# An RG-LRU and attention trunk: another order of the first loads, squares and adds, and the first block's convolution by halves

## The chip, the cores and the metric

The kernel runs on 1 core of a Trainium2 chip. The metric is the device time of one execution in microseconds (us); lower is better. The engines are TensorE (PE; weight loads are listed as PEld), VectorE (DVE), ScalarE (ACT), GpSimd (POOL) and SyncE (SP), whose queue issues nearly all DMAs.

## The reference

One sequence of 1024 positions, width 1024, float32, goes through two pre-norm residual layers. The change lies in the first, the RG-LRU layer, of width 1536 in 12 blocks of 128:

```python
def rms_norm(x, g):
    y = xf * lax.rsqrt(jnp.mean(xf * xf, axis=-1, keepdims=True) + EPS)
    return (y * g).astype(x.dtype)

def lru_mixer(h, w_in, conv_w, conv_b, wa, ba, wx, bx, a_param, w_out):
    u = h @ w_in
    xb, gate = u[..., :LRU_WIDTH], u[..., LRU_WIDTH:]
    xc = causal_depthwise_conv(xb, conv_w, conv_b)      # 4 taps
    r = jax.nn.sigmoid(block_diag_linear(xc, wa, ba))
    i = jax.nn.sigmoid(block_diag_linear(xc, wx, bx))
    log_a = -LRU_C * r * jax.nn.softplus(-a_param)
    a = jnp.exp(log_a)
    bterm = jnp.sqrt(-jnp.expm1(2.0 * log_a)) * (i * xc)
    _, hs = lax.associative_scan(combine, (a, bterm), axis=1)
    return (hs * jax.nn.silu(gate)) @ w_out
```

The second layer is forgetting attention with 16 heads of 64; the change does not touch its code.

## The kernel before, in words

Everything is held transposed: features on the 128 partitions, positions along a row. The 1024 positions are two halves of 512 (`halves`); x is 16 tiles `xs[h][k]` of 128x512, 256 KB each, h the half and k one of KT = 8 feature tiles. A printed name as x03 is half 0, k = 3. Precision is kept by splitting: each x tile, scaled by the norm's g (gnt), becomes hh (cast on ACT) and hl (the rest, on VectorE, L242); each weight tile of 128x512 (four k) becomes wh (cast on ACT, L88) and wl (the rest, L99, on VectorE or POOL). A product is three matmuls per k: hh with wh, hh with wl, hl with wh.

The norm's factor is applied after the products. `square_x` squares the x tiles on ACT (L252) and adds them up in m2 (`acc`, L254; the buffers of the squares are the later tiles th and ti); `first_row(h)` multiplies m2 by ones into row, takes the root on ACT (L261) and the reciprocal on VectorE (L262): rs. Then us = ups times rs (`conv`, L279), xc = four taps of us (one on ACT, L280, three on VectorE, L283), xch and xcl its split; `gates` multiplies those with the split gate weights wgh and wgl; `softplus` is a chain of operations on 128x12 values on VectorE that ends with c2 and nc2, which `recur` reads on ACT (L329, L330); `silu` scales gps by rs, takes tanh and writes sg; `recur` scans; `outputs` splits the result into yh and yl, and `project_out` multiplies them with the output weights (ops) and adds into x.

The loop runs over the 12 blocks. Block 0 makes its u product (ups) and its gate product (gps) while x is still arriving; block 1 makes ups for both halves with the row of the second half between; later blocks use two-bank PSUM tiles (tag S, two of them), so the third block's ups (ups_549 before) takes the place that block 0's ups or gps held. Loads come in the order of the string in the loop over steps (n gnt, u and g half a weight column of 256 KB each, x one x tile, p the small parameters pct); all go through SP's queue in order.

The order on each engine is not the order of the code: a tile scheduler interleaves the instructions by its own costs and due times, and each engine then works through its queue in order. `issue_after` holds instructions back until a named one is issued.

Of the kernel before, what the change touches and what calls it, by code (L numbers as in the profile page):

```python
# [11 lines left out]
F32 = mybir.dt.float32  # L12
F32R = mybir.dt.float32r
BF16 = mybir.dt.bfloat16
AF = mybir.ActivationFunctionType
ALU = mybir.AluOpType

P = 128
SEQ = 1024
HALF = 512  # L20
KT = 8
NB = 12
# [16 lines left out]
def trunk(ctx: ExitStack, tc: tile.TileContext, xt, w0, wg, wo0, pc, gn, gf, w1, wv, wf, bf, wo1, out):  # L39
    nc = tc.nc  # L40

    def pool(name, bufs, **kw):
        return tc.tile_pool(name=name, bufs=bufs, **kw)
# [2 lines left out]
    const.tile([P, 32], F32, name="pad0")  # L46
    ctx.enter_context(pool("edge", 1, side="right")).tile([P, 56], F32, name="pad1")
    dram = ctx.enter_context(pool("dram", 1, space=DRAM))
    ctx.enter_context(pool("gap", 1)).tile([P, 24], F32, name="pad2")
    hpool = ctx.enter_context(pool("hT", 16))  # L50
    wpool = ctx.enter_context(pool("w", 4))
    ps = ctx.enter_context(pool("ps", 2, space=PSUM))
# [45 lines left out]
    def to_lo(lo, src, hi, eng):  # L98
        return eng.tensor_tensor(lo, src, f32(hi), ALU.subtract)  # L99
# [14 lines left out]
    def weights(src, parts=wpool, lo_eng=nc.gpsimd):  # L114

        for k in range(0, src.shape[1], 4):
            n = min(4, src.shape[1] - k)
            yield from split_weights([(src[:, k : k + n], slice(0, P))], (n, P), nc.scalar, lo_eng, parts)
# [13 lines left out]
    def drain(gen):  # L132
        for _ in gen:
            pass
# [45 lines left out]
    with ExitStack() as l0:  # L180
# [8 lines left out]
        def long(tag, dtype=F32, bufs=1):  # L189
            return tmp.tile([P, SEQ], dtype, tag=tag, name=tag, bufs=bufs)  # L190
# [28 lines left out]

        xs = [[xpool.tile([P, HALF], F32, name=f"x{h}{k}") for k in range(KT)] for h in range(2)]  # L220
        first = ([], [])
        early = [weights(w0[0], lo_eng=nc.vector), weights(w0[NB], lo_eng=nc.gpsimd)]
        k = 0
        for step in "nuxxgxuxgxxpxxxxxxxxxx":
            if step == "n":
                nc.sync.dma_start(gnt, gn)
            elif step == "p":
                nc.sync.dma_start(pct, pc)
            elif step in "ug":
                first["ug".index(step)].extend(itertools.islice(early["ug".index(step)], 4))  # L230
            else:
                nc.sync.dma_start(xs[k // KT][k % KT], xt[k // KT, :, k % KT])
                k += 1
# [3 lines left out]
        def split_x(h, layer=0):  # L237
            for k, (hi, lo) in enumerate((raw, hT)[layer][h]):
                g_ = gnt[:, layer, k : k + 1]
                x = xs[h][k]  # L240
                to_hi(hi, x, nc.scalar, scale=g_)
                nc.vector.scalar_tensor_tensor(lo, x, g_, f32(hi), ALU.mult, ALU.subtract)  # L242
                yield
# [4 lines left out]
        def square_x(h):  # L248
            to = acc[:, halves[h]]
            for k in range(KT):  # L250
                z = sq[k % 4] if k else to
                nc.scalar.activation(z, xs[h][k], AF.Square)  # L252
                if k:
                    nc.vector.tensor_tensor(to, to, z, ALU.add)  # L254
                yield

        def first_row(h):
# [6 lines left out]
        def rms_row(parts, rs, *rms):  # L264
            return inv_rms(parts, ps.tile([P, HALF], F32, tag="O", name="sscol")[:, : HALF // P], rs, *rms)

        for _ in zip(split_x(0), square_x(0)):
            pass


# [2 lines left out]
        def product(pt, h, w):  # L273
            gemm(pt, zip(w, raw[h]))

        def conv(n, ups):
            us, xc = long("us"), long("xc", bufs=2)
            for pt, cs in zip(ups, halves if len(ups) == 2 else (slice(0, SEQ),)):
                nc.vector.tensor_tensor(us[:, cs], pt, rs[:, cs], ALU.mult)  # L279
            nc.scalar.activation(xc, us, AF.Identity, bias=cb[:, n : n + 1], scale=cw[3][:, n : n + 1])  # L280
            for d in range(1, 4):
                w_ = cw[3 - d][:, n : n + 1]
                tap = nc.vector.scalar_tensor_tensor(xc[:, d:], us[:, : SEQ - d], w_, xc[:, d:], ALU.mult, ALU.add)  # L283
            xh, xl = long("xch", F32R), long("xcl", F32R)
            to_hi(xh, xc, nc.scalar)
            to_lo(xl, xc, xh, nc.vector)
            wt = wpool.tile([P, 4, P], F32, tag="wf", name="wgf", bufs=3)[:, :2]
            nc.sync.dma_start(wt, wg[n])
            wgh = tmp.tile([P, 2, P], F32R, tag="wgh", name="wgh")
            wgl = tmp.tile([P, 2, P], F32R, tag="wgl", name="wgl")  # L290
            to_hi(wgh, wt, nc.vector)
            to_lo(wgl, wt, wgh, nc.vector)
            state[n] = dict(xc=xc, x=(xh, xl), w=(wgh, wgl), tap=tap)

        def gates(n):

# [81 lines left out]
        for n in range(NB):  # L378
# [14 lines left out]
            if n == 0:  # L393
                gps = held[0] = two_banks("gps")
                product(gps[:, 0], 0, first[1])
                first_row(0)
                for _ in zip(split_x(1), square_x(1)):
                    pass
            else:
                gates(n - 1)  # L400
                if n > 1:
                    with tc.issue_after(state[n - 1]["last"].ins):
                        outputs(n - 2)
            product(ups[1], 1, wu)
            if n == 0:
                row, rooted, done = first_row(1)
                product(gps[:, 1], 1, first[1])
                both = ups
            conv(n, both)
            if n == 0:  # L410
                with tc.issue_after(rooted.ins), tc.issue_after(done.ins):
                    softplus()
                drain(silu(state[0], held.pop(0)))
            if n % 2 and n > 1:
                fill = itertools.chain(fill, project_out((n - 3) // 2))
            take(fill, 4)
# [684 lines left out]
```

## Time and profile before

| what | value |
|---|---|
| median of three runs | 1130.3 us (1128.25 to 1131.4) |
| the profiled execution | 1132.74 us, its span 1130.9 us |
| TensorE busy | 1112.0 us, 98% of the span |
| VectorE, ACT, POOL busy | 67%, 52%, 15% |
| mean granted TensorE clock | 0.995 |
| read from HBM | 63.30 MB |

The profile is of one execution. Its rows give start, duration, engine, line, operation and tiles by the program's names; what stands in brackets is the idle time ahead of an instruction and what ended it. Overlapping matmuls are shown with their whole duration, so the spacing of their starts is the rate. A row that ends in x2 stands for two instructions that follow each other, with the time from the first's start to the last's end.

### The profile page before, as it was taken

Reading aid. Unit: us, or ns where it says so; the run is one execution under the profiler, and the core shown is the slowest. Engines: PE = TensorE matmul, PEld = TensorE weight load, DVE = VectorE, ACT = ScalarE, POOL = GpSimd, SP = SyncE. Lnnn points to the kernel's source line nnn. Section 1 sums busy time; section 2 is a strip of 40 time slices with the busy share of each in tenths; the row PEclk is TensorE's granted clock in tenths of the full one; section 3 lists DMA queues with packets and bytes.
Section 4 is the critical chain, followed back from the end, with each engine's and each line's share of the span. In section 5 each row is a group of like instructions: output and inputs, shape, how many; then the busy total and the mean of one; then the engine's idle time right before and its main releaser. Section 6 shows DMA issues by size and latency. Waiting matters only on the chain.

```text
span 1130.9 us, 15754 instructions
## 1 busy us (share of the span) xinstructions
PE 1112.0 (98%) x5681; PEld 937.3 (83%) x5681; DVE 762.2 (67%) x1271; ACT 589.6 (52%) x1077; POOL 165.6 (15%) x105
## 2 busy tenths in 40 slices
PE   9999999999999999999999999999999999999997
PEld 7786888888888887988888888888888888878886
DVE  7789756876568789666676466763666645676645
ACT  8387445354453666455555355553555534554435
POOL 1312112121121202330110100101001010010110
PEclk9999999999999999999999999999999999999999
DMA  6111121111211114443334124252142421665445
GB/s 216 52 42 52 43 61 38 52 52 42 61 37 52 56 57 144 124 123 103 99 89 119 52 84 109 75 123 62 58 120 85 110 81 52 182 180 157 151 149 186
DMA packets 63702, 105.43 MB, mean 93 GB/s; under 512 B 9508, under 2 KB 24484, under 8 KB 63624
## 3 DMA queue, kind: packets, MB, share of 16 engines
q1 hardware_dynamic: 63624, 104.42, 31.3%
q8 instruction: 45, 0.74, 0.3%
q14 instruction: 33, 0.27, 0.1%
HBM read 63.30 MB, written 15.93 MB: 70 GB/s over the span
## 4 chain that ended last, share of the span: by engine, by line
PE 87%; DVE 4%; ACT 2%; DMA 2%; issue 2%; POOL 1%; SPq 0%; POOLq 0%; ACTq 0%
PE gps L57 32%; PE ops L57 15%; PE ups L57 10%; PE vps L57 7%; PE S L57 6%; PE O L57 6%; PE pt L61 5%; PE turn L57 3%; PE gate L57 2%; POOL wl L99 1%; DMA wf<-in_w 1%; DVE sq L167 1%; ACT wh L88 1%; DVE x L470 0%; DMA x<-in_xt 0%
## 5 line engine op out<-in xcount | busy, mean ns | idle before, releaser
L57 PE MATMUL gps<-hh,wh 128*128 128x512 f32 x576 | 228.6, 397 | 1.0 <-DVE qkl L582 1.0
L57 PE MATMUL gps<-hl,wh 128*128 128x512 f32 x576 | 226.0, 392 | 0.0
L57 PE MATMUL gps<-hh,wl 128*128 128x512 f32 x576 | 226.0, 392 | 0.0
L88 ACT CAST wh<-wf 128x512 fp32r<-128x512 f32 (+2 forms) x156 | 94.6, 607 | 146.6 <-PE gps L57 49.2
L707 ACT ACTIVATE p<-S,m 128x128 f32<-128x128 f32 (+7 forms) x128 | 94.9, 741 | 135.2 <-DVE m L702 134.1
L99 POOL TENSOR_TENSOR wl<-wf,wh 128x512 fp32r<-128x512 f32 (+1 forms) x60 | 100.7, 1685 | 389.4 <-ACT wh L88 332.5
L99 DVE TENSOR_TENSOR pl<-pt,ph 128x512 fp32r<-128x512 f32 (+1 forms) x198 | 98.8, 540 | 81.7 <-ACT ph L88 81.3
L57 PEld LDWEIGHTS gps<-hl,wh 128*128 128x128 f32 x576 | 108.4, 188 | 23.8
L57 PEld LDWEIGHTS gps<-hh,wh 128*128 128x128 f32 x576 | 108.6, 189 | 20.2 <-DVE qkl L582 1.2
L57 PEld LDWEIGHTS gps<-hh,wl 128*128 128x128 f32 x576 | 108.9, 189 | 19.7 <-POOL wl L99 0.7
L702 DVE CUSTOM_DVE_ANT_0 S<-S,mask 128x128 f32<-128x128 f32 (+7 forms) x128 | 97.3, 761 | 30.2 <-PE S L57 25.8
L734 POOL TENSOR_TENSOR sg<-sg,recb 64x1024 f32<-64x1024 f32 (+1 forms) x17 | 38.8, 2282 | 460.8 <-DMA recb<-recd 400.8
L88 ACT CAST ph<-pt 128x512 fp32r<-128x512 f32 (+1 forms) x198 | 83.6, 473 | 30.6 <-PE pt L61 25.3
L57 PE MATMUL S<-T,U 96*128 96x512 f32 (+7 forms) x384 | 91.7, 348 | 2.4 <-ACT p L707 2.4
L99 DVE TENSOR_TENSOR wl<-wf,wh 128x512 fp32r<-128x512 f32 x96 | 70.0, 733 | 26.5 <-ACT wh L88 25.8
L369 DVE TENSOR_TENSOR x<-x,ops 128x512 f32<-128x512 f32 x80 | 54.1, 682 | 48.1 <-PE ops L57 48.1
L57 PEld LDWEIGHTS S<-T,U 128*128 128x128 f32 (+1 forms) x384 | 68.3, 189 | 15.6 <-ACT p L707 3.6
L61 PE MATMUL pt<-ident,p 128*128 128x128 f32 x576 | 79.4, 273 | 0.0
L57 PE MATMUL ups<-hh,wh 128*128 128x512 f32 x192 | 76.6, 400 | 1.7 <-ACT hh L90 1.0
L61 PEld LDWEIGHTS pt<-ident,p 128*128 128x128 f32 x576 | 67.4, 141 | 12.4 <-issue 2.2
L57 PE MATMUL vps<-wh,hh 128*128 128x256 f32 (+1 forms) x256 | 74.6, 292 | 3.0 <-DVE sg L673 2.1
L57 PE MATMUL ups<-hh,wl 128*128 128x512 f32 x192 | 76.0, 396 | 1.5 <-POOL wl L99 1.5
(176 smaller groups left out, 2260.0 us busy)
## 6 DMA issues: line engine op xcount, KB each, us to landing
wf<-in_w SPq DMA_DIRECT2D x100, 256.0 KB
wf<-in_wo SPq DMA_DIRECT2D x64, 128.0 KB
U<-qkh SPq DMA_DIRECT2D x64, 128.0 KB
T<-qkh SPq DMA_DIRECT2D x28, 256.0 KB
x<-in_xt SPq DMA_DIRECT2D x16, 256.0 KB
x1d<-x SPq DMA_DIRECT2D x16, 256.0 KB
wf<-in_wv SPq DMA_DIRECT2D x16, 256.0 KB
U<-qkl SPq DMA_DIRECT2D x32, 128.0 KB
```

The source lines that it names most:

```text
L57: pe[0] = nc.tensor.matmul(*args, **kw)
L61: pe[0] = nc.tensor.transpose(*args)
L88: nc.scalar.copy(hi, src)
L99: return eng.tensor_tensor(lo, src, f32(hi), ALU.subtract)
L167: eng.tensor_tensor(parts[0], parts[0], sq, ALU.add)
L369: nc.vector.tensor_tensor(x, x, pt, ALU.add)
L702: nc.vector.tensor_tensor_reduce(S[:, :n], S[:, :n], mask[:, SEQ - n :], -1.0, -NEG, ALU.add, ALU.min, accum_out=m)
L707: seen[0] = nc.scalar.activation(p, S[:, :n], AF.Exp, bias=m, scale=-1.0, accum_out=sums[:, i : i + 1])
L734: nc.gpsimd.tensor_tensor(sg, sg, recs[hd // 2][rows, cs], ALU.mult)
```

## The change

1. pad2 is 40 floats wide instead of 24, which moves the tiles placed behind it by 64 bytes in each partition.
2. The wl tiles of block 0's gate weights are made by VectorE instead of POOL.
3. The loads come in another order: g's first half ahead of x01, u's and g's second halves behind x03, pct last.
4. Splitting the first half's x is no longer interleaved with squaring it: the first half is split, then the second half is split with the first half squared, then the second half is squared, then the first half's row follows. The first half's adds are on POOL; the second's stay on VectorE.
5. Block 0's convolution and silu are done by halves: taps, xch and xcl 512 wide each; the silu is held back until the second root is issued. Taps are in a function of their own (`taps`), used by all blocks.

The instructions are as many as before but for the halves; on TensorE the same matmuls stand in another order in the first 900 or so.

```diff
--- before.py
+++ after.py
@@ -46,7 +46,7 @@
     const.tile([P, 32], F32, name="pad0")
     ctx.enter_context(pool("edge", 1, side="right")).tile([P, 56], F32, name="pad1")
     dram = ctx.enter_context(pool("dram", 1, space=DRAM))
-    ctx.enter_context(pool("gap", 1)).tile([P, 24], F32, name="pad2")
+    ctx.enter_context(pool("gap", 1)).tile([P, 40], F32, name="pad2")
     hpool = ctx.enter_context(pool("hT", 16))
     wpool = ctx.enter_context(pool("w", 4))
     ps = ctx.enter_context(pool("ps", 2, space=PSUM))
@@ -219,9 +219,9 @@
 
         xs = [[xpool.tile([P, HALF], F32, name=f"x{h}{k}") for k in range(KT)] for h in range(2)]
         first = ([], [])
-        early = [weights(w0[0], lo_eng=nc.vector), weights(w0[NB], lo_eng=nc.gpsimd)]
+        early = [weights(w0[0], lo_eng=nc.vector), weights(w0[NB], lo_eng=nc.vector)]
         k = 0
-        for step in "nuxxgxuxgxxpxxxxxxxxxx":
+        for step in "nuxgxxxugxxxxxxxxxxxxp":
             if step == "n":
                 nc.sync.dma_start(gnt, gn)
             elif step == "p":
@@ -251,7 +251,7 @@
                 z = sq[k % 4] if k else to
                 nc.scalar.activation(z, xs[h][k], AF.Square)
                 if k:
-                    nc.vector.tensor_tensor(to, to, z, ALU.add)
+                    (nc.vector if h else nc.gpsimd).tensor_tensor(to, to, z, ALU.add)
                 yield
 
         def first_row(h):
@@ -264,7 +264,7 @@
         def rms_row(parts, rs, *rms):
             return inv_rms(parts, ps.tile([P, HALF], F32, tag="O", name="sscol")[:, : HALF // P], rs, *rms)
 
-        for _ in zip(split_x(0), square_x(0)):
+        for _ in split_x(0):
             pass
 
 
@@ -273,24 +273,37 @@
         def product(pt, h, w):
             gemm(pt, zip(w, raw[h]))
 
-        def conv(n, ups):
+        def conv(n, ups, parts=(slice(0, SEQ),)):
             us, xc = long("us"), long("xc", bufs=2)
+            xh, xl = long("xch", F32R), long("xcl", F32R)
             for pt, cs in zip(ups, halves if len(ups) == 2 else (slice(0, SEQ),)):
                 nc.vector.tensor_tensor(us[:, cs], pt, rs[:, cs], ALU.mult)
-            nc.scalar.activation(xc, us, AF.Identity, bias=cb[:, n : n + 1], scale=cw[3][:, n : n + 1])
-            for d in range(1, 4):
-                w_ = cw[3 - d][:, n : n + 1]
-                tap = nc.vector.scalar_tensor_tensor(xc[:, d:], us[:, : SEQ - d], w_, xc[:, d:], ALU.mult, ALU.add)
-            xh, xl = long("xch", F32R), long("xcl", F32R)
-            to_hi(xh, xc, nc.scalar)
-            to_lo(xl, xc, xh, nc.vector)
+                if len(parts) < len(ups):
+                    continue
+                taps(n, us, xc, cs)
+            if len(parts) < len(ups):
+                taps(n, us, xc, parts[0])
+            for cs in parts:
+                to_hi(xh[:, cs], xc[:, cs], nc.scalar)
+                to_lo(xl[:, cs], xc[:, cs], xh[:, cs], nc.vector)
             wt = wpool.tile([P, 4, P], F32, tag="wf", name="wgf", bufs=3)[:, :2]
             nc.sync.dma_start(wt, wg[n])
             wgh = tmp.tile([P, 2, P], F32R, tag="wgh", name="wgh")
             wgl = tmp.tile([P, 2, P], F32R, tag="wgl", name="wgl")
             to_hi(wgh, wt, nc.vector)
             to_lo(wgl, wt, wgh, nc.vector)
-            state[n] = dict(xc=xc, x=(xh, xl), w=(wgh, wgl), tap=tap)
+            state[n] = dict(xc=xc, x=(xh, xl), w=(wgh, wgl), tap=last_tap[0])
+
+        last_tap = [None]
+
+        def taps(n, us, xc, cs):
+            nc.scalar.activation(xc[:, cs], us[:, cs], AF.Identity, bias=cb[:, n : n + 1], scale=cw[3][:, n : n + 1])
+            for d in range(1, 4):
+                w_ = cw[3 - d][:, n : n + 1]
+                to = slice(max(cs.start, d), cs.stop)
+                last_tap[0] = nc.vector.scalar_tensor_tensor(
+                    xc[:, to], us[:, to.start - d : to.stop - d], w_, xc[:, to], ALU.mult, ALU.add
+                )
 
         def gates(n):
 
@@ -393,9 +406,11 @@
             if n == 0:
                 gps = held[0] = two_banks("gps")
                 product(gps[:, 0], 0, first[1])
+                for _ in zip(split_x(1), square_x(0)):
+                    pass
+                for _ in square_x(1):
+                    pass
                 first_row(0)
-                for _ in zip(split_x(1), square_x(1)):
-                    pass
             else:
                 gates(n - 1)
                 if n > 1:
@@ -406,11 +421,12 @@
                 row, rooted, done = first_row(1)
                 product(gps[:, 1], 1, first[1])
                 both = ups
-            conv(n, both)
+            conv(n, both, halves if n == 0 else (slice(0, SEQ),))
             if n == 0:
                 with tc.issue_after(rooted.ins), tc.issue_after(done.ins):
                     softplus()
-                drain(silu(state[0], held.pop(0)))
+                with tc.issue_after(rooted.ins):
+                    drain(silu(state[0], held.pop(0), halves))
             if n % 2 and n > 1:
                 fill = itertools.chain(fill, project_out((n - 3) // 2))
             take(fill, 4)
```

How the change moves instructions. First the start: VectorE from its first wl on, before; hl is named with the x tile that it is made of, m2 is the sum of squares.

```order
L99 TENSOR_TENSOR wl_138<-wf_136,wh_137 128x512
L242 SCALAR_TENSOR_TENSOR hl_179<-x00_119,gnt_101,hh_178 128x512
L242 SCALAR_TENSOR_TENSOR hl_181<-x01_120,gnt_101,hh_180 128x512
L254 TENSOR_TENSOR m2_210<-m2_210,th_211 128x512
L242 SCALAR_TENSOR_TENSOR hl_183<-x02_121,gnt_101,hh_182 128x512
L254 TENSOR_TENSOR m2_210<-m2_210,ti_212 128x512
L99 TENSOR_TENSOR wl_153<-wf_151,wh_152 128x512
L242 SCALAR_TENSOR_TENSOR hl_185<-x03_122,gnt_101,hh_184 128x512
```

The same place in the changed program:

```order
L99 TENSOR_TENSOR wl_138<-wf_136,wh_137 128x512
L242 SCALAR_TENSOR_TENSOR hl_179<-x00_119,gnt_101,hh_178 128x512
L99 TENSOR_TENSOR wl_145<-wf_143,wh_144 128x512
L242 SCALAR_TENSOR_TENSOR hl_181<-x01_120,gnt_101,hh_180 128x512
L242 SCALAR_TENSOR_TENSOR hl_183<-x02_121,gnt_101,hh_182 128x512
L242 SCALAR_TENSOR_TENSOR hl_185<-x03_122,gnt_101,hh_184 128x512
L99 TENSOR_TENSOR wl_154<-wf_152,wh_153 128x512
L99 TENSOR_TENSOR wl_160<-wf_158,wh_159 128x512
L242 SCALAR_TENSOR_TENSOR hl_187<-x04_123,gnt_101,hh_186 128x512
```

The adds into m2 have gone from between the hl tiles, and the gate weights' wl stand there, one at x01, one behind x03. POOL at the same place, before:

```order
masks.py:199 AFFINE_SELECT ident_78<-ident_78 128x128
L99 TENSOR_TENSOR wl_146<-wf_144,wh_145 128x512
L99 TENSOR_TENSOR wl_160<-wf_158,wh_159 128x512
L99 TENSOR_TENSOR wl_427<-wf_425,wh_426 128x512
L99 TENSOR_TENSOR wl_433<-wf_431,wh_432 128x512
```

and after:

```order
masks.py:199 AFFINE_SELECT ident_78<-ident_78 128x128
L254 TENSOR_TENSOR m2_210<-m2_210,th_211 128x512
L254 TENSOR_TENSOR m2_210<-m2_210,ti_212 128x512 x2
L254 TENSOR_TENSOR m2_210<-m2_210,th_211 128x512 x2
L254 TENSOR_TENSOR m2_210<-m2_210,ti_212 128x512 x2
L99 TENSOR_TENSOR wl_436<-wf_434,wh_435 128x512
```

POOL's two wl of block 0 are gone, and the seven adds into m2 stand ahead of the wl of block 1 (wl_427 before, wl_436 now).

Second, the second row's reciprocal: VectorE from there to us of block 0's second half, before; hba, hbx and sp_d are 128x12 values of the softplus and of biases.

```order
L262 RECIPROCAL rs_177<-rs_177 128x512
L216 TENSOR_SCALAR hba_117<-pct_100 128x12
L217 TENSOR_SCALAR hbx_118<-pct_100 128x12
L204 TENSOR_SCALAR sp_d_115<-sp_e_114 128x12
L279 TENSOR_TENSOR us_381<-ups_244,rs_177 128x512
L313 TENSOR_TENSOR gps_269<-gps_269,rs_177 128x1024
```

After:

```order
L304 SCALAR_TENSOR_TENSOR xc_382<-us_381,pct_100,xc_382 128x509
L99 TENSOR_TENSOR xcl_384<-xc_382,xch_383 128x512
L262 RECIPROCAL rs_177<-rs_177 128x512
L216 TENSOR_SCALAR hba_117<-pct_100 128x12
L217 TENSOR_SCALAR hbx_118<-pct_100 128x12
L328 SCALAR_TENSOR_TENSOR sg_427<-sg_427,gps_254 128x512
L204 TENSOR_SCALAR sp_d_115<-sp_e_114 128x12
L280 TENSOR_TENSOR us_381<-ups_229,rs_177 128x512
L326 TENSOR_TENSOR gps_254<-gps_254,rs_177 128x512
```

The taps and xcl of the first half stand ahead of the reciprocal now, and sg of the first half (the silu) between it and us. On TensorE, the last matmuls ahead of the third block's ups (ups_549), which needs the bank that us frees; before:

```order
L57 MATMUL ups_438<-hl_207,wh_432 128x512
L57 MATMUL ups_438<-hh_208,wh_432 128x512
L57 MATMUL ups_438<-hh_208,wl_433 128x512
L57 MATMUL ups_438<-hl_209,wh_432 128x512
L57 MATMUL ups_549<-hh_178,wh_538 128x512
```

After, where the third block's ups is ups_558:

```order
L57 MATMUL ups_446<-hl_193,wh_441 128x512
L57 MATMUL gate_474<-xch_383,wgh_401 128x512
L57 MATMUL gate_474<-xch_383,wgl_402 128x512
L57 MATMUL gate_474<-xcl_384,wgh_401 128x512
L57 MATMUL ups_558<-hh_178,wh_547 128x512
```

Behind the second row 20 matmuls of block 1 stood ahead of it; now there are 12, and three matmuls of block 0's gates.

Third, the end of the softplus on VectorE (its last row is nc2), before:

```order
L283 SCALAR_TENSOR_TENSOR xc_510<-us_509,pct_100,xc_510 128x1021
L210 SCALAR_TENSOR_TENSOR sp_q_116<-sp_q_116,sp_d_115 128x12
L279 TENSOR_TENSOR us_625<-ups_549,rs_177 128x1024
L210 SCALAR_TENSOR_TENSOR sp_q_116<-sp_q_116,sp_d_115 128x12
L211 SCALAR_TENSOR_TENSOR sp_q_116<-sp_q_116,sp_e_114 128x12
L212 TENSOR_SCALAR sp_d_115<-pct_100 128x12
L213 SCALAR_TENSOR_TENSOR sp_d_115<-sp_q_116,sp_d_115 128x12
L214 TENSOR_SCALAR c2_112<-sp_d_115 128x12
L215 TENSOR_SCALAR nc2_113<-sp_d_115 128x12
```

After:

```order
L304 SCALAR_TENSOR_TENSOR xc_519<-us_518,pct_100,xc_519 128x1021
L211 SCALAR_TENSOR_TENSOR sp_q_116<-sp_q_116,sp_e_114 128x12
L212 TENSOR_SCALAR sp_d_115<-pct_100 128x12
L213 SCALAR_TENSOR_TENSOR sp_d_115<-sp_q_116,sp_d_115 128x12
L214 TENSOR_SCALAR c2_112<-sp_d_115 128x12
L215 TENSOR_SCALAR nc2_113<-sp_d_115 128x12
L280 TENSOR_TENSOR us_634<-ups_558,rs_177 128x1024
```

us of the third block (us_625 before, us_634 now) stood ahead of the last operations of the softplus, and stands behind them now.

## The prediction

> **What bounds the kernel now.** I read the page first (engine shares, slices, the chain that ended last), then the waits of TensorE in the stretch that the change reaches, then a table by stage, then the timeline of the gaps. From the page:
>
> ```profile
> span 1130.9 us, 15754 instructions
> ...
> PE 1112.0 (98%) x5681; PEld 937.3 (83%) x5681; DVE 762.2 (67%) x1271; ACT 589.6 (52%) x1077; POOL 165.6 (15%) x105
> ...
> PE 87%; DVE 4%; ACT 2%; DMA 2%; issue 2%; POOL 1%; SPq 0%; POOLq 0%; ACTq 0%
> ```
>
> TensorE is busy 98% of the span and 87% of the last chain. The number of its matmuls does not change, so the time can only move where TensorE stands still, or where its clock is held down. The waits of TensorE in the first 110 us, which holds all rows whose order on TensorE the change alters:
>
> ```profile
> PE ups L57 <- POOL wl L99: 1.5, 1, 1.5
> ...
> PE ups L57 <- ACT hh L90: 1.0, 1, 1.0
> PE ops L57 <- ACT yh L88: 0.7, 1, 0.7
> PE ups L57 <- DVE us L279: 0.4, 1, 0.4
> PE ops L57 <- DVE yl L99: 0.2, 1, 0.2
> ```
>
> Three places, then: the start, one wait near 45 us, and a group near 100 us. The table by stage (after the busy times stand granted clock, DMA share, GB/s) adds the clock:
>
> ```profile
> 10.70:13.40 2.70, 2.70 (x7) 2.14 (x7) 2.70 (x5) 2.70 (x6) 0.88 (x1) 0.50 1.03 370
> ...
> 98.00:105.60 7.60, 5.12 (x20) 2.86 (x19) 7.60 (x9) 7.54 (x10) 4.53 (x2) 1.00 0.05 17
> 105.60:109.10 3.50, 3.50 (x10) 2.73 (x9) 3.50 (x5) 0.61 (x1) 1.41 (x1) 0.51 0.45 148
> ```
>
> The clock is at half (0.50, 0.51) in two stretches, each right after TensorE had gaps. Spacing is 0.23 us at full clock, 0.43 at half:
>
> ```profile
> 12.13 0.63 PE L57 MATMUL gps<-hh,wl 128*128 128x512 f32 x1
> 12.56 0.63 PE L57 MATMUL gps<-hl,wh 128*128 128x512 f32 x1
> ...
> 17.55 0.39 PE L57 MATMUL gps<-hh,wl 128*128 128x512 f32 x1
> 17.78 0.39 PE L57 MATMUL ups<-hl,wh 128*128 128x512 f32 x1
> ```
>
> The half-clock stretch at 105.6 runs about 3.4 us: 8 matmuls where 15 would fit, 7 x 0.23 = 1.6 us lost. One such stretch is 1.6 us below.
>
> **The change, part by part.** My sum is made against the profiled execution, 1132.74 us (span 1130.9 and 1.84 around it). The three timed runs have median 1130.3, so that execution is 2.4 us above it.
>
> *(a) The start.* The rows that price it:
>
> ```profile
> 5.78 0.79 PE L57 MATMUL ups<-hh,wh 128*128 128x512 f32 x1
> 7.38 0.72 ACT L90 ACTIVATE hh<-x,gnt 128x512 fp32r<-128x512 f32 x1 [1.14 <-DMA x<-in_xt]
> 8.80 0.69 DVE L254 TENSOR_TENSOR m<-m,th 128x512 f32<-128x512 f32 x1
> 9.22 1.42 POOL L99 TENSOR_TENSOR wl<-wf,wh 128x512 fp32r<-128x512 f32 x1 [7.90 <-ACT wh L88]
> 9.67 0.61 ACT L252 ACTIVATE ti<-x 128x512 f32<-128x512 f32 x1
> 9.79 1.39 DVE L242 SCALAR_TENSOR_TENSOR hl<-x,gnt,hh 128x512 fp32r<-128x512 f32 x1 [0.30 <-ACT hh L90]
> 11.84 0.60 ACT L88 CAST wh<-wf 128x512 fp32r<-128x512 f32 x1
> 12.31 0.74 DVE L242 SCALAR_TENSOR_TENSOR hl<-x,gnt,hh 128x512 fp32r<-128x512 f32 x1
> 21.86 1.02 PE L57 MATMUL row<-m,onesf 128*128 128x512 f32 x2
> 22.94 0.39 PE L57 MATMUL ups<-hh,wh 128*128 128x512 f32 x1
> 33.31 2.38 DVE L254 TENSOR_TENSOR m<-m,ti 128x512 f32<-128x512 f32 x2
> 33.40 3.43 POOL L99 TENSOR_TENSOR wl<-wf,wh 128x512 fp32r<-128x512 f32 x2 [2.90 <-DVE us L279]
> 40.20 1.29 POOL L99 TENSOR_TENSOR wl<-wf,wh 128x512 fp32r<-128x512 f32 x1 [3.37 <-ACT wh L88]
> ```
>
> The first three loads stay, so the first product starts at 5.78 as before. The fourth load is now a half of g's weights instead of x01. ACT waited for that slot until 7.38; its cast (0.60) lets g's first product start at about 8.0. The next slot is 256 KB at 370 GB/s, 0.7 us, later: x01 at 8.1, its hh (0.72) at 8.8. From there TensorE has six matmuls per x tile, 6 x 0.23 = 1.36 us, and could run on. That ordering alone is a gain.
>
> Against it stands where the squares are added. VectorE loses seven adds of the first half and gains two wl; POOL gets the seven adds and loses two wl. A POOL operation of two inputs of 128x512 takes 1.29 us alone. Beside VectorE's two-input operations both are slowed: an hl of 0.74 took 1.39 under the wl at 9.22, and two adds of 0.69 took 2.38 beside two wl that took 3.43. That is 3.43/2 = 1.7 us for a POOL operation and a VectorE operation together. The Trainium skill says the same in "SBUF — State Buffer", section "Who interferes with whom": a VectorE instruction with two SBUF inputs contends with a GpSimd instruction that reads SBUF, through a shared read interface. By that rule the moved adds cost VectorE time although they left its queue; the trace agrees, 1.39 against 0.74 us.
>
> The first add on POOL can start once the second square is there: 8.8 + 0.61, about 9.4. Squares come faster than one in 1.7 us, so seven pairs run until 9.4 + 7 x 1.7 = 21.3. VectorE's queue beside them is hl of x02 and x03, two wl, then hl of x04, x05, x06: one in each pair. The last product of x04 so waits until 17.9, of x05 until 19.6, of x06 until 21.3. From x06's on, 18 matmuls lie ahead of the row: 18 x 0.23 = 4.1, row at 25.4. In before the row comes six matmuls earlier, at 21.86, and it costs 0.85 (1.08 to the matmul at 22.94, less one spacing); with six more the same state is at 24.3. After has it at 25.4 + 1.08 = 26.5. I take **+2.1**. If nothing is slowed, the row follows from the wait for x04's hl at about 14.9: 30 matmuls later, 21.7, total 22.8: **-1.5**. If the two engines exclude each other wholly (1.29 + 0.66 = 1.95 a pair), seven pairs give 23.1, and 1.8 more: **+3.9**. I stay with the middle since the pair at 33.31 is the nearest row.
>
> *(b) The clock there.* With waits around 13 to 18 us, after has a stretch as gappy as those ahead of the two half-clock stretches. **+1.0** (0 to 1.6). In the Trainium skill, "TensorE: Matmul & The Clock Gate", Part 1, the throttle looks at free-running windows of 3413 ns; the rows at half clock agree with that length (about 3.4 us), and it would make this cost appear in some executions only.
>
> *(c) The wait near 45 us.*
>
> ```profile
> 39.08 1.02 PE L57 MATMUL row<-m,onesf 128*128 128x512 f32 x2
> 40.13 0.69 ACT L261 ACTIVATE rs<-row,epst 128x512 f32<-128x512 f32 x1
> 40.85 3.35 DVE L262 RECIPROCAL rs<-rs 128x512 f32<-128x512 f32 x1 [5.17 <-ACT rs L261]
> 44.28 0.68 DVE L279 TENSOR_TENSOR us<-ups,rs 128x512 f32<-128x512 f32 x1
> 45.12 0.47 PE L57 MATMUL ups<-hh,wh 128*128 128x512 f32 x1 [0.44 <-DVE us L279]
> ```
>
> The third block's first product needs the bank that us frees: row to there takes 45.12 - 39.08 = 6.04. It is covered by 0.85 of the row and 20 matmuls: 5.4, so 0.6 is lost. In after only 12 matmuls of the second block and 3 gate matmuls stand between: 0.85 + 15 x 0.23 = 4.25. And one sg operation of the silu, now by halves, stands on VectorE between reciprocal and us: 0.66, by the hl form. Chain 6.7, wait 2.45 instead of 0.65: **+1.8**. It follows from the order alone. A wait of 2.45 in 3.4 may halve the clock too: **+0.8** (0 to 1.6).
>
> *(d) The group near 100 us.*
>
> ```profile
> 62.43 1.25 ACT L329 ACTIVATE m<-th,c 128x1024 f32<-128x1024 f32 x1 [1.02 <-DVE nc L215]
> 65.93 1.23 DVE L332 SCALAR_TENSOR_TENSOR m<-th,m 128x1024 f32<-128x1024 f32 x1 [3.52 <-ACT th L331]
> 99.58 0.50 PE L57 MATMUL ops<-yh,wh 128*128 128x512 f32 x1 [0.66 <-ACT yh L88]
> 101.07 5.94 POOL L99 TENSOR_TENSOR wl<-wf,wh 128x512 fp32r<-128x512 f32 x2 [15.01 <-ACT wh L88]
> 102.51 0.73 PE L57 MATMUL ops<-yl,wh 128*128 128x512 f32 x2 [0.17 <-DVE yl L99]
> 104.78 0.51 PE L57 MATMUL ups<-hh,wl 128*128 128x512 f32 x1 [1.53 <-POOL wl L99]
> ```
>
> Idle 0.66 + 0.17 + 1.53 = 2.4, and each of the three restarts costs the overlap of two matmuls (0.39 - 0.23 = 0.16): 2.9. These are waits for ACT, VectorE and POOL that come late, and they come late because VectorE stood idle for 3.52 ahead of 65.93, for an ACT that waited at 62.43 for the last operation of the softplus (nc). In after, half of gps, of three taps and of xcl of the first block is done ahead of the second reciprocal, and us of the third block stands behind nc: with about 0.65 for a half (0.68 to 0.74 in the rows above), 5 x 0.65 + 1.3, some 4.5 us, less lies between the second reciprocal and nc. TensorE needs as long as before from the second row to this group: 8 matmuls fewer, 1.8, and the longer wait of (c), 1.8. So the other engines come here some 4 us earlier against waits of 2.9; slack about 1. **-2.9** (0 if they stay), and the half-clock stretch behind them goes too: **-1.6** in this execution.
>
> *(e) The rest.* Wider pad: 64 bytes of shift for the tiles behind it; no row shows a price for it: 0, -1 to +1. Convolution and silu by halves add a few instructions to VectorE and ACT, which have 33% and 48% to spare, in a stretch where POOL and VectorE aren't waited for except in (c): 0. pct loads last instead of twelfth, 0.1 us of transfer, and its first user comes after 30 us: 0.
>
> **Sum:** 2.1 + 1.0 + 1.8 + 0.8 - 2.9 - 1.6 = +1.2 on the profiled execution: 1133.9. Against the median, which is 2.4 lower and so hardly had every half-clock stretch, I count half of the last term: +2.0, 1132.3. Between them I forecast **1133.0**.
>
> **Rivals.** *The adds on POOL hide.* Then (a) is -1.5 and (b) 0: 1.8 + 0.8 - 2.9 - 1.6 - 1.5 = -3.4, without the new half clock in (c) -4.2: 1126.1 to 1129.3, say 1126.9 from the median. For it: no product waits for an add, only the row does. Against: 1.39 for 0.74. Chance 0.17.
>
> *The group near 100 us stays (slower).* The place is POOL's wl at 101.07: two of them took 5.94 us where 1.29 each is the price alone, beside VectorE's yl and xcl. In after the order of yl, xcl and this wl is the same. The slack of about 1 us decides: if less than 3 of the 4 us of lead arrive, because some other wait of ACT or VectorE takes the place of the one for nc, the group keeps its waits and the half-clock stretch. Then (d) is 0: 2.1 + 1.0 + 1.8 + 0.8 = +5.7, 1136.0 on the median, 1138.4 on the profiled execution. Chance 0.25.
>
> *Whole exclusion at the start, or one half-clock stretch more.* +1.8: with the forecast 1134.8, with the last stretch kept, 1136.4. Chance 0.08.
>
> **How the numbers follow.** What this measurement can tell from no change is about 0.3%, 3.4 us: faster is under 1126.9, slower over 1133.7. My forecast has 0.50: 0.03 faster, 0.29 same, 0.18 slower. First rival 0.12, 0.05, 0. Second 0, 0.02, 0.23. Third all slower, 0.08. Sums: 0.15, 0.36, 0.49. The range is 1127.0 to 1138.5: below it most of the first rival (0.11), above it the ends of the other two (0.08). The forecast's own range is 1130 to 1136.
>
> **What would show it.** Right: the row of the first half near 25 us or later, hl and wl of VectorE at 1.4 instead of 0.7 beside POOL's adds of 1.7; idle of TensorE near 2.3 us ahead of the third block's first product, put down to us; no wait for yh, yl or POOL's wl at the third block's output products. Wrong: adds of 1.3 us on POOL and a row before 22.5; waits at the third block as long as before.

## The result, and the profile after

The changed kernel takes 1135.22 us (median of 7 runs, 1131.91 to 1136.83), the kernel before 1129.82 (7 runs beside it): a ratio of 1.0049, 95% interval 1.0031 to 1.0066. It is slower by 5.4 us, where the prediction said 1133.0 in a range of 1127.0 to 1138.5, with slower as its likeliest case. The profiled execution of the changed kernel is its quickest of the seven: 1131.91 us, span 1130.1. So the two profiles alone show hardly any difference, and where the rest of the 5.4 us is has to come from the runs.

The waits of TensorE in the first 115 us of the changed kernel (in total, times, longest):

```profile
PE ups L57 <- DVE us L280: 2.8, 1, 2.8
PE ups L57 <- ACT hh L90: 1.3, 2, 0.9
PE ups L57 <- DVE hl L242: 1.2, 1, 1.2
...
PE ups L57 <- POOL wl L99: 0.5, 2, 0.3
PE gps L57 <- DVE wl L99: 0.5, 1, 0.5
```

The group near 100 us (yh, yl, POOL's wl) is gone but for two short waits for POOL's wl (0.28 and 0.21 us); the wait for us has grown from 0.4 to 2.8; at the start there are waits for hl and wl of VectorE that were not there. The timeline of the start:

```profile
9.01 1.33 POOL L254 TENSOR_TENSOR m<-m,th 128x512 f32<-128x512 f32 x1 [7.69 <-ACT th L252]
...
12.51 3.49 DVE L99 TENSOR_TENSOR wl<-wf,wh 128x512 fp32r<-128x512 f32 x2
...
13.82 3.30 POOL L254 TENSOR_TENSOR m<-m,th 128x512 f32<-128x512 f32 x2
...
15.92 7.81 DVE L242 SCALAR_TENSOR_TENSOR hl<-x,gnt,hh 128x512 fp32r<-128x512 f32 x7
...
16.05 0.49 PE L57 MATMUL gps<-hh,wl 128*128 128x512 f32 x1 [0.49 <-DVE wl L99]
...
17.21 3.32 POOL L254 TENSOR_TENSOR m<-m,ti 128x512 f32<-128x512 f32 x2
...
17.73 0.50 PE L57 MATMUL ups<-hl,wh 128*128 128x512 f32 x1 [1.19 <-DVE hl L242]
...
19.43 0.50 PE L57 MATMUL ups<-hl,wh 128*128 128x512 f32 x1
...
21.13 0.50 PE L57 MATMUL ups<-hl,wh 128*128 128x512 f32 x1
...
25.36 1.02 PE L57 MATMUL row<-m,onesf 128*128 128x512 f32 x2
```

POOL's adds come at 3.3 us for two, and VectorE's operations follow in step: two wl in 3.49 us where 0.69 is the price of one. TensorE's products with hl start at 17.73, 19.43, 21.13, one in 1.7 us, and the row at 25.36. The place near 50 us:

```profile
43.04 1.02 PE L57 MATMUL row<-m,onesf 128*128 128x512 f32 x2
...
44.82 3.35 DVE L262 RECIPROCAL rs<-rs 128x512 f32<-128x512 f32 x1 [2.24 <-ACT rs L261]
...
47.60 1.26 POOL L99 TENSOR_TENSOR wl<-wf,wh 128x512 fp32r<-128x512 f32 x1 [3.88 <-ACT wh L88]
48.09 0.81 DVE L216 TENSOR_SCALAR hba<-pct 128x12 f32<-128x12 f32 x1
...
48.88 0.67 DVE L328 SCALAR_TENSOR_TENSOR sg<-sg,gps 128x512 f32<-128x512 f32 x1
...
49.55 0.68 DVE L280 TENSOR_TENSOR us<-ups,rs 128x512 f32<-128x512 f32 x1
...
50.29 0.80 PE L57 MATMUL ups<-hh,wh 128*128 128x512 f32 x1 [2.78 <-DVE us L280]
```

From row to the third block's first product it is 7.25 us, before 6.04. sg stands between, and hba, 12 values a partition, takes 0.81 us beside POOL's wl. The clock by stages (the last three columns are granted clock, DMA share, GB/s):

```profile
9.00:12.30 3.30, 3.30 (x9) 2.53 (x9) 2.92 (x3) 3.30 (x7) 3.13 (x3) 0.50 1.04 399
49.90:53.20 3.30, 2.91 (x7) 2.36 (x8) 3.27 (x9) 1.30 (x2) 0.00 (x0) 0.50 0.21 78
53.20:112.00 58.80, 58.31 (x256) 47.66 (x255) 53.68 (x63) 44.81 (x51) 11.83 (x6) 1.00 0.13 41
```

The half-clock stretch behind the group near 100 us is gone, and one stands behind the wait for us instead. The profile before has a third half-clock stretch, from about 778 to 781 us (clock 0.52), in the second layer; the prediction's table ended ahead of it. After has none there. The first matmul into vps, early in the second layer, starts at 458.96 us before and at 459.14 after. So in this pair of profiles, with two half-clock stretches in the first layer of each, the change makes the first layer hardly longer.

### The profile page after: what moved, and what is told of

The parts are those of the page before. It is cut to its first block, busy times and chain, and to the rows that moved or that the text cites. A ratio compares the mean times of both kernels' runs of the same rounds, so it can differ in the third digit from the quotient of the medians.

```text
span 1130.1 us, 15760 instructions
## 1 busy us (share of the span) xinstructions
PE 1107.8 (98%) x5681; PEld 936.0 (83%) x5681; DVE 765.2 (68%) x1272; ACT 590.3 (52%) x1080; POOL 172.4 (15%) x110
## 4 chain that ended last, share of the span: by engine, by line
PE 85%; DVE 5%; DMA 4%; issue 2%; ACT 2%; POOL 1%; SPq 0%; ACTq 0%; DVEq 0%; POOLq 0%
PE gps L57 30%; PE ops L57 15%; PE ups L57 10%; PE vps L57 7%; PE S L57 6%; PE O L57 6%; PE pt L61 5%; PE turn L57 3%; PE gate L57 2%; DMA x<-in_xt 1%; DMA wf<-in_w 1%; POOL wl L99 1%; ACT wh L88 1%; DMA yhl<-y1d 0%; DVE wl L99 0%
## 5 line engine op out<-in xcount | busy, mean ns | idle before, releaser
L99 POOL TENSOR_TENSOR wl<-wf,wh 128x512 fp32r<-128x512 f32 (+1 forms) x58 | 95.4, 1650 | 375.7 <-ACT wh L88 280.3
L99 DVE TENSOR_TENSOR wl<-wf,wh 128x512 fp32r<-128x512 f32 x98 | 73.7, 757 | 27.0 <-ACT wh L88 26.0
L57 PE MATMUL ups<-hl,wh 128*128 128x512 f32 x192 | 76.3, 397 | 1.3 <-DVE hl L242 1.2
```

The costliest lines, as they stand in the source:

```text
L57: pe[0] = nc.tensor.matmul(*args, **kw)
```

## The experiments

Each is timed against the kernel before on the same chip. Beside its time stands the granted clock as a mean over its runs, each run's being given to 0.001. In those batches the kernel before had 1128.2 to 1128.4 us and a clock of 0.9975 (27 runs), 0.9987 (17) and 0.9974 (18). Kernels of different batches are compared by their ratios to it.

**Adds back on VectorE.**

```diff
-                    (nc.vector if h else nc.gpsimd).tensor_tensor(to, to, z, ALU.add)
+                    nc.vector.tensor_tensor(to, to, z, ALU.add)
```

> The changed kernel (1135.2 us) with one line undone: the first half's squares are added by VectorE again; loads, wl and the halves stay. My theory: the start is slow because VectorE's two-input operations and POOL's adds take 1.7 us a pair. So hl and wl of VectorE go back to 0.7 us, the row of the first half comes near 22.5 us instead of 25.4, the wait at 45 us (2.8) and the absent waits near 100 us stay as they are, and the time falls by 2 to 3 us, to about 1132.5. Rival (the throttle by itself, whose windows fall by chance on gaps): the row may move, but the time stays at 1135 unless the granted clock changes. Rival (the new order of loads and casts is what costs): row stays near 25, time 1135.

Measured: 1127.18 us, ratio 0.9988 (0.9980 to 0.9997), clock 0.9976. By the ratios (1.0049 and, measured again below, 1.0053 against 0.9988) one line is worth about 7 us, and the kernel is now a little faster than before. VectorE at the start of this kernel, and its two rows and third block on TensorE:

```profile
12.77 1.29 DVE L99 TENSOR_TENSOR wl<-wf,wh 128x512 fp32r<-128x512 f32 x2
13.97 0.75 DVE L242 SCALAR_TENSOR_TENSOR hl<-x,gnt,hh 128x512 fp32r<-128x512 f32 x1
14.64 0.69 DVE L254 TENSOR_TENSOR m<-m,th 128x512 f32<-128x512 f32 x1
...
21.63 1.02 PE L57 MATMUL row<-m,onesf 128*128 128x512 f32 x2
...
40.67 1.02 PE L57 MATMUL row<-m,onesf 128*128 128x512 f32 x2
...
47.92 0.50 PE L57 MATMUL ups<-hh,wh 128*128 128x512 f32 x1 [2.79 <-DVE us L280]
```

With seven adds more in its queue VectorE is quicker: two wl take 1.29 us instead of 3.49, hl 0.75. The second row, at the same place of TensorE's order in both, comes at 40.67 instead of 43.04: 2.4 us, what the theory expected. That is the figure of one pair of profiles: in the second profile of the changed kernel, below, this row comes at 45.45, behind two half-clock stretches. The wait for us stays 2.79, and here no half-clock stretch follows it. The other 4 to 5 us of the 7 are not in these waits; the clock, 0.9976 against 0.994, is where they must be looked for (0.0036 of 1130 us is 4 us).

**Convolution and silu whole again.**

```diff
-            conv(n, both, halves if n == 0 else (slice(0, SEQ),))
+            conv(n, both)
...
-                    drain(silu(state[0], held.pop(0), halves))
+                    drain(silu(state[0], held.pop(0)))
```

> The changed kernel with the first block's convolution and silu whole again (also for the silu's parts); the adds stay on POOL. My theory: the start stays (row near 25.4), the wait ahead of the third block's first product falls from 2.8 to about 0.6 us, and the waits near 100 us that the changed kernel lost come back (yh, yl, POOL's wl, together about 2.4 us idle). Sum: -1.8 - 0.8 + 2.9 + 0.8 = +1, about 1136. Rival (the halves are what makes the changed kernel slow, by the wait at 45 us alone): -2.6, 1132.6.

Measured: 1132.13 us, ratio 1.0035 (1.0023 to 1.0048), clock 0.9958. Row to the third block's product is 6.04 us again. The wait there is 1.1 us where 0.6 was expected, since 17 matmuls stand between instead of 20, and the first row comes at 27.0 where 25.4 was expected, behind two half-clock stretches. The group near 100 us is back, with a wait for VectorE's wgl in the place of the one for POOL's wl:

```profile
103.50 0.50 PE L57 MATMUL ops<-yh,wh 128*128 128x512 f32 x1 [0.55 <-ACT yh L88]
106.68 0.74 PE L57 MATMUL gate<-xch,wgl 128*128 128x512 f32 x2 [1.50 <-DVE wgl L99]
107.81 0.73 PE L57 MATMUL ops<-yl,wh 128*128 128x512 f32 x2 [0.16 <-DVE yl L99]
```

The sum was wrong: by the ratios this kernel is 1.6 to 2.0 us faster than the changed one, not 1 slower (the intervals overlap a little). That is the way of the rival, though not by its reason, since the waits near 100 us did come back. The clock, 0.9958 against 0.994, is worth about 2 us by itself (0.0018 x 1130).

**Both undone: loads, wl, squares behind, pad alone.**

> The changed kernel with both undone: adds of the first half on VectorE, convolution and silu whole. Left are the new order of loads, the wl of the gate weights on VectorE, the squares behind the split, and the wider pad. My theory: the start is no worse than before the change (row near 22.5 with six matmuls more or fewer), the wait at 45 us is 0.6, the waits near 100 us are there as before: 1129 to 1130.5, the time of before. Rival (the order of loads or the pad costs by itself): 1132 or more.

Measured: 1127.97 us, ratio 0.9992 (0.9982 to 1.0001), clock 0.9969: no difference from before that can be measured. The new order of loads and casts is worth nothing clear by itself and costs nothing. The group near 100 us is there (0.65, 0.17 and 1.53 us), so that the changed kernel lacks the waits for yh and yl comes from the halves.

**The old pad.**

> The changed kernel with the pad at its old width of 24 floats, nothing else. My theory: no row has a price for it, 1135.2 within 1 us, with rows of the same durations. Rival (placement matters): 2 us or more off, seen in matmul spacing or DMA times.

Measured: 1136.92 us, ratio 1.0074 (1.0057 to 1.0091), clock 0.993. Unclear against 1.0049 and 1.0053 of the changed kernel; taken up again in the last pair.

**The changed kernel again.**

> The changed kernel itself, beside the next three on the same chip. Its granted clock over all runs is 0.994 so far where the kernel before has 0.9975; my theory puts about 4 of its 6 us on that. Expected: 1135, clock 0.994 again. Rival (that clock was of one chip or chance): clock 0.997, time 1131.

Measured: 1134.35 us, ratio 1.0053 (1.0040 to 1.0066), clock 0.994 (0.993 to 0.995 in five runs). The low clock is this kernel's. Its second profile shows what the first did not:

```profile
17.00:23.80 6.80, 5.62 (x13) 4.46 (x14) 6.80 (x7) 6.80 (x13) 3.80 (x3) 0.50 0.31 111
...
1017.20:1020.40 3.20, 3.20 (x8) 2.53 (x9) 1.82 (x4) 0.67 (x2) 0.00 (x0) 0.50 0.50 135
```

Behind the start's waits TensorE ran at half clock for 6.8 us, two stretches in a row, with 13 matmuls in them. The first row came at 27.8 in this execution, and the first matmul into vps at 461.8. The wait for us is 2.78 as before, and this time no half-clock stretch follows it. One wait of the group near 100 us is back, the longer of two for POOL's wl:

```profile
PE ups L57 <- POOL wl L99: 1.6, 2, 1.3
```

**Work for TensorE in the wait for us.** Eleven matmuls that nobody reads ahead of the first gate product.

```diff
+                    if n == 0 and j == 0 and cs.start == 0:
+                        for _ in range(11):
+                            matmul(pt, first[0][0][0], raw[0][0][0], start=True, stop=True)
                     gemm(pt, [(w, tuple(z[:, cs] for z in s["x"]))])
```

> The changed kernel with 11 more matmuls that nobody reads (2.5 us) ahead of the first block's first gate product, so that TensorE has work in the 2.8 us ahead of the third block's first product. That product still waits for the same us, so at a given clock nothing gets faster. Clock theory: the half-clock stretch that can follow this gap no longer comes; clock up by about 0.001, time 1 us less (1134). Rival (the clock does not follow this gap): time and clock as the changed kernel, or a little slower by the extra work.

Measured: 1131.52 us, ratio 1.0032 (1.0020 to 1.0043), clock 0.996. Useless work made the kernel 2.8 us faster than beside it on the same chip. The third block's product still stands behind us, with 0.3 us idle ahead of it, 7.3 us after the row. So in this kernel the gap costs more than its own length, by a lower clock (0.994 with it, 0.996 without). Not every such gap does so: five profiles have this wait of 2.8 us with nothing in it, and a half-clock stretch follows it in two of them, the first of the changed kernel and that of the copies below. With the adds back on VectorE the same wait goes with a clock of 0.9976.

**Work for TensorE in the waits at the start.**

```diff
+                fl = ps.tile([P, HALF], F32, tag="O", name="fl")
+                for k, c in ((4, 5), (5, 1), (6, 1)):
+                    for _ in range(c):
+                        matmul(fl, first[0][0][0], raw[0][k][0], start=True, stop=True)
                 product(gps[:, 0], 0, first[1])
```

> The changed kernel with 7 more matmuls that nobody reads in the waits of TensorE at the start (5 ahead of the wait for the fourth tile's wl and hl, 1 in each of the next two). They also leave ten matmuls of the second block between the second row and the third block's first product (25 instead of 15). Clock theory: row near 25.4 as in the changed kernel, since POOL and VectorE still set it; the wait at 45 us falls from 2.8 to under 0.5 (2.3 us); no half-clock stretch behind the start's waits, clock 0.997 instead of 0.994 (3 us): 1130. Rival (the start's waits don't bring the low clock): clock 0.994 to 0.995, 1132.7.

Measured: 1127.72 us, ratio 0.9995 (0.9987 to 1.0004), clock 0.9975 (11 runs). The row comes at 25.62, the adds and hl as slow as in the changed kernel, and between 13 and 24 us the clock is full. The wait for us is gone: the ten matmuls cover 2.3 us of it, and hba takes 0.11 us instead of 0.81 in this profile, where no operation of POOL lies beside it. The kernel is 6.6 us below the changed one: about 2.7 by the wait, and about 0.0035 x 1130 = 4.0 by the clock, an estimate that holds if TensorE has work all through the half-clock stretches. Both waits were closed at once here, so this run alone does not say which of them brought the clock up.

**What of POOL's add it is.** In two kernels the adds are replaced, to see which operation of POOL holds VectorE up.

```diff
-                    (nc.vector if h else nc.gpsimd).tensor_tensor(to, to, z, ALU.add)
+                    if h:
+                        nc.vector.tensor_tensor(to, to, z, ALU.add)
+                    else:
+                        nc.gpsimd.tensor_scalar(to, z, 1.0, 0.0, ALU.mult, ALU.add)  # copy
+                        nc.gpsimd.memset(z, 1.0)  # or, in the other kernel, this alone
```

> The changed kernel with each of POOL's seven adds replaced by a copy of the new square into m2 (one input instead of two; the sum is left out, so the norm's factor of the first half comes from one tile alone). All waits stay the same. If what slows VectorE is POOL reading on-chip memory at all while VectorE reads two tiles, hl beside the copies still takes about 1.4 us instead of 0.74 and the fourth tile's product comes late as before (near 17 us). If it takes two inputs on POOL too, hl goes back to 0.74.

> The changed kernel with each of POOL's seven adds replaced by a memset of the square's buffer after it is written (no input; the sum is left out, so the norm's factor of the first half comes from one tile alone). POOL has seven operations of 128x512 at the same places, but reads nothing. If reading is what contends, hl takes 0.74 us beside them and the fourth tile's product comes about 3 us earlier than in the changed kernel (near 14.5 us). Rival (any POOL instruction beside VectorE, or VectorE's longer queue by two wl, is what delays): hl 1.4 us again, or the product late all the same.

Measured, the copies (one run, 1132.72 us):

```profile
11.81 0.62 POOL L257 TENSOR_SCALAR m<-ti 128x512 f32<-128x512 f32 x1 [0.51 <-ACT ti L252]
...
13.49 0.73 DVE L242 SCALAR_TENSOR_TENSOR hl<-x,gnt,hh 128x512 fp32r<-128x512 f32 x1
13.98 0.73 POOL L257 TENSOR_SCALAR m<-th 128x512 f32<-128x512 f32 x1 [1.55 <-ACT th L252]
14.47 0.77 DVE L242 SCALAR_TENSOR_TENSOR hl<-x,gnt,hh 128x512 fp32r<-128x512 f32 x1 [0.25 <-ACT hh L90]
```

and the memsets (one run, 1130.93 us):

```profile
15.91 4.82 DVE L242 SCALAR_TENSOR_TENSOR hl<-x,gnt,hh 128x512 fp32r<-128x512 f32 x7
16.46 0.53 POOL L257 MEMSET ti<- 128x512 f32 x1 [0.60 <-ACT ti L252]
17.60 0.53 POOL L257 MEMSET ti<- 128x512 f32 x1 [0.61 <-ACT ti L252]
```

With two memsets inside their stretch seven hl take 4.82 us, 0.69 each. In the changed kernel the first three of the seven took 5.16 us beside the adds, and the other four, behind the last add, 0.66 each. So it is not any POOL instruction, nor VectorE's longer queue. (The row is early there, since m2 is one tile's square, and its reciprocal stands ahead of hl; the kernel's time says little.) The copies do not settle the other half: a copy takes 0.62 us, half an add, and mostly falls between two hl. At 13.98 one lies under two hl and takes 0.73, with hl at 0.73 and 0.77: little is lost, but the overlap is only about 0.2 us on each side. Whether one input on POOL would hold VectorE up as two do stays open.

**The silu whole, adds on VectorE, halves of the convolution kept.**

> The kernel with the first half's adds on VectorE (1127.2) and the first block's silu whole, so that no sg stands between the second reciprocal and us; convolution by halves stays, and one more matmul stands between row and third block. My theory: row to third block's first product falls from 7.25 to about 6.1 us, the wait from 2.8 to 1.5; the waits near 100 us stay away: 1126. Rival (the waits near 100 us come back since the silu's rest now stands ahead of the softplus): 1128 or more.

Measured: 1124.39 us, ratio 0.9967 (0.9954 to 0.9979), clock 0.9972, better than either kernel.

```profile
39.11 1.02 PE L57 MATMUL row<-m,onesf 128*128 128x512 f32 x2
...
44.16 0.11 DVE L216 TENSOR_SCALAR hba<-pct 128x12 f32<-128x12 f32 x1
...
44.32 0.68 DVE L280 TENSOR_TENSOR us<-ups,rs 128x512 f32<-128x512 f32 x1
...
45.06 0.50 PE L57 MATMUL ups<-hh,wh 128*128 128x512 f32 x1 [1.26 <-DVE us L280]
```

From row to product it is 5.95 us instead of 7.25, near the 6.1 that was expected. Only about half of that is sg, which took 0.67: hba takes 0.11 here instead of 0.81, since POOL's wl begins only at 44.58. There is no wait near 100 us.

**More cover for what is left of that wait, and the pad once more.**

```diff
-                take(steps, 2)
+                take(steps, 1)
```

> The kernel with the first half's adds on VectorE and the silu whole (1124.4), and one line more: of the second block's first product one pair of x tiles instead of two is left free ahead of the second row, so that 21 matmuls instead of 16 stand between that row and the third block's first product. My theory: that product still comes 6.0 us after the row, covered by 0.85 + 21 x 0.23 = 5.6: the idle falls from 1.26 to 0.2 or 0.3 us, the time by 1.1: 1123.3, clock no lower. Rival (the matmuls taken from ahead of the row leave a gap there, or the wait moves): no gain, 1124.4 or more.

> The same kernel with the pad at its old width of 24 floats. The changed kernel with that pad measured 1.0074 of the kernel before, the changed kernel itself 1.0049 and 1.0053, so the width may be worth up to 2 us. My theory (placement has no price): the same time within 0.7 us. Rival: 1 to 2 us slower.

Measured: 1124.33 us, ratio 0.9962 (0.9946 to 0.9978), and with the old pad 1125.68, ratio 0.9976 (0.9966 to 0.9987). The waits of TensorE in the first of the two:

```profile
PE ups L57 <- POOL wl L99: 1.0, 1, 1.0
...
PE ups L57 <- DVE us L280: 0.2, 1, 0.2
```

The wait for us fell to 0.2 us as expected, and no time came of it: a wait of 1.0 us for POOL's wl near 100 us is back. With more work ahead of it TensorE comes sooner to the next thing that is late. The old pad is 1.4 us slower here and was, by the ratios, 2.4 to 2.8 us slower above. In each pair the intervals overlap, so a small gain of the wider pad is possible and not shown; that both pairs point the same way speaks for it. No row of the profiles that I compared shows where it would be.

## Why the prediction was right or wrong, point by point

**(a), the adds on POOL: right, the row to a tenth by luck.** The products that wait for hl were put at 17.9, 19.6 and 21.3, the row at 25.4; they came at 17.73, 19.43, 21.13 and 25.36. The value taken, 1.7 us a pair, was the right one of the three: the adds take 3.3 for two. Undoing the line gave 2.4 us at the second row, where the sum had 2.1. The start went otherwise than told in small things: TensorE's first product came at 6.55 instead of 5.78, behind a load, and the first add at 9.01 instead of 9.4. And in four other profiles with this start the row came between 26.3 and 27.8, behind half-clock stretches. The memsets show that a POOL operation that reads nothing does not slow VectorE. That agrees with the rule of "SBUF — State Buffer", "Who interferes with whom", in the Trainium skill, which names POOL's reading as the condition. The rival that the adds hide is refuted by the rows: 1.7 us for hl and wl beside them, 0.65 to 0.75 without.

**(b) and the clock in (c): the mechanism was right for the start, the size was not.** This is the term that was mis-sized. The sum had +1.0 and +0.8 for new half-clock stretches and -1.6 for the one that goes, +0.2 in all. Over their runs the changed kernel has 0.994 and the kernel before 0.9974 to 0.9987. The difference of 0.0034 to 0.0047 is at most 4 to 5 us of 1130, an estimate that takes TensorE to have work all through the stretches. I counted one stretch at most behind each gap; the second profile has two in a row behind the start's waits. My reading, which no run tests by itself, is that a TensorE that gets six matmuls in 1.7 us from VectorE does not fill a stretch even while no single wait is long.

That the start brings the low clock, the profiles show together. Five have the adds on POOL and nothing in the waits at the start (the changed kernel twice, convolution and silu whole, the old pad, the filled wait for us). Four of them have one or two half-clock stretches between 16 and 24 us, and their kernels' clocks are 0.993 to 0.996. The six with the adds on VectorE, the kernel before among them, have none there, nor has the one with matmuls in the start's waits; their clocks are 0.997 to 0.9987. It is not the whole account: in half of the fourteen profiles, with the change and without, a half-clock stretch or two lie in the second layer, and the copies, one run at 0.991, have none between 16 and 24 us but five elsewhere. For the wait for us the evidence is weaker. Filling it raised the clock from 0.994 to 0.996, but with the adds on VectorE the clock is 0.9976 with a wait of 2.79 us and 0.9972 with one of 1.26.

For the two profiled executions the sum was 2.0 us too high (1133.9 forecast, 1131.91 measured). The third half-clock stretch of before, near 780 us, which the sum did not know of and after does not have, is 1.7 us (half of 3.4). That the rest then agrees is luck in part: the first layer ended 0.2 us later, not 1.0, and in the second layer TensorE waits 1.2 us longer in after for ACT's p, which the change does not touch.

**(c) right, a little too small.** The wait was put at 2.45 us and is 2.8, the way from row to product at 6.7 and is 7.25. sg is in it as told (0.67). The 0.5 us that was missed is hba, which in before took 0.11 and here 0.81, ending with POOL's wl beside it.

**(d) right for yh and yl; the slack held in one execution of two.** The waits for yh and yl are gone: the kernels without the halves have them in their profiles, those with them do not. The same holds for the half-clock stretch behind the group, which all three profiles without the halves have and none with them. Of POOL's 1.53 us, 0.28 is left in the first profile of the changed kernel but 1.35 in the second, and 1.34 with the old pad. So the slack of about 1 us did not suffice each time, and the rival that the group stays, at 0.25, came in part.

**(e) mostly right.** The order of loads by itself cannot be told from nothing (0.9982 to 1.0001 of before). Whether the pad is worth nothing or 1 to 3 us stays open.

So the time moved the way that was told. By the rows of the first pair the waits cost about 2.5 us net (2.1 at the start, 2.3 at us, less 1.9 near 100 us). The first layer as a whole ended 0.2 us later in that pair and 2.8 us later in the second profile, so the share of the waits is known only as 0 to 3 us. The rest of the 5.4 us goes with the clock, whose share was thought to be near nothing and is 4 to 5 us at most.

## What to carry to other kernels

Moving an addition off the busy engine is no relief if it then runs beside that engine's two-input operations: count the pair, not the queue. Waits of TensorE that come close together may cost as much again by the half clock behind them, in some executions and not in others, so compare the granted clock of all runs, not of one profile. A wait that cannot be closed may be worth filling with matmuls that nobody reads. And where a wait is closed by giving TensorE other work first, look at what it reaches sooner.

## What the runs showed of the hardware that was not expected

A 128x12 operation of one input on VectorE (hba) took 0.80 to 0.84 us instead of 0.11 in six profiles, each time ending with a POOL subtraction of 128x512 that had begun before it (in the changed kernel 47.60 + 1.26 = 48.86 against 48.09 + 0.81 = 48.90). In the two profiles with more cover, where that subtraction ended sooner, it took 0.23 and again ended with it, and in the six with none beside it 0.11. So it looks as if not only VectorE's two-input operations are held up by POOL. The Trainium skill lists tensor_scalar, in the same section of "SBUF — State Buffer", among the operations that can take the shared pair of ports; no run here tested this one alone. On POOL an operation of one input and 128x512 takes 0.62 us, of two inputs 1.29, a memset 0.53. And eleven matmuls of no use made a kernel faster by 2.8 us.
